# The last row of each partition of a final store, sent by nine small DMAs of 96 to 1 rows

## The chip, the cores and the metric

One core of a Trainium2 chip. The metric is device time in microseconds (us) of one execution, a median of several. All runs used here are fast, with a granted clock of 1.00. The experiments ran on two chips (6 and 11 in the record), each beside the kernel before on the same chip. A ratio is the mean time of one kernel's fast runs over that of the kernel before in the same rounds, so it is not quite the ratio of the medians quoted beside it.

## The reference

RMS normalisation with a gain and a ReLU, over 16,384 rows of 512 float32:

```python
def reference(x, gamma, eps):                       # x: 16 x 1024 x 512
    rms = np.sqrt(np.mean(x ** 2, axis=-1, keepdims=True) + eps)
    return np.maximum(x / rms * gamma, 0).astype(np.float32)
```

33.6 MB have to be read and 33.6 MB written, and little is computed on each element.

## The kernel before

The rows are cut into eight chunks of 4 MB. In a chunk each of 128 partitions (the rows of the memory on the chip) holds K = 16 neighbouring rows, so 32 KB lie together both in a partition and in the output. Six slots hold six chunks; the last two chunks reuse slots 0 and 1 after their stores have landed. SyncE issues every large load and store. ScalarE squares and sums, VectorE scales and clips in place. The parts that matter here:

```python
    K = 16
    nchunks = rows // K          # 8
    nslots = 6
    ov = out2.rearrange("(c p k) d -> c p k d", p=P, k=K)
    # ...
    def store(i):
        nc.sync.dma_start(out=ov[i], in_=slot_ap(i)).then_inc(sem_slot[i % nslots], 16)
    # ...
        for i in range(nchunks):
            nc.sync.wait_ge(done, per * (i + 1))
            store(i)
            # ... (load of the chunk that reuses a slot)
    # ... the end of the program: SyncE waits for every slot's last store
        nc.sync.reg_mov(landed, 64)
        for s in range(nchunks - nslots):
            nc.sync.wait_ge(sem_slot[s], landed)
```

A store here adds 16 to its semaphore (a counter on which an engine can wait): in the trace before, the last store shows 16 landings on it, the last at 159.88 us, 0.48 after the last of its packets had ended (159.40). I call the count that one DMA engine adds for one store an **increment**: in the records it is a packet of 4 bytes, 9 ns long, behind that engine's data.

## Time and profile before

| | before |
|---|---|
| device time, median of the first 3 runs | 162.86 us (162.81 to 163.07) |
| span of the profiled execution (its device time) | 160.9 us (162.69 us) |
| VectorE busy | 126.0 us |
| data moved, mean rate | 67.1 MB, 417 GB/s |
| last store issued / landed | 146.46 / 159.88 us |

The issue of the last store in the timeline (start, length, engine, line) took 0.33 us, where its data landed 13.4 us after its start:

```profile
146.46 0.33 SPq L87 DMA_DIRECT2D out_dram<-slots  x1
```

The DMA view of the stretch from 159.3 us to the end has one packet left, the increment of the engine that ends last:

```profile
DMA packets 1, 0.00 MB, mean 0 GB/s; under 512 B 1, under 2 KB 1, under 8 KB 1
```

"Under 512 B" counts increments here, since the data packets of this store have 32,768 bytes each. So the end is one engine's: its last data packet, its increment (over at 159.40 us), and then the 0.48 us until the increment lands. The prediction shows how the other fifteen lie before it.

### The profile page before, as it was taken

The page shows a single profiled execution, that of the slowest core. Times are in us where ns is not written, and L with a number is a line of the kernel's source. Part 1 is how long each engine was busy: PE and PEld are TensorE (multiplying, and loading weights), DVE is VectorE, ACT ScalarE, POOL GpSimd, SP SyncE. Part 2 cuts the span into 40 slices and gives each one's busy share as a digit, 9 for nine tenths or more (in the row PEclk, how much of TensorE's full clock was granted, in tenths as well). Part 3 has the DMA queues.
Part 4 walks back from the last instruction along what each step waited for, and adds up shares of the span by engine and source line. Part 5 has one row for each costly group of instructions (what it writes and reads, how often), then busy time and mean ns, then how long its engine had stood idle before and what let it go on. Part 6 is the DMA issues. An engine that isn't in the chain of part 4 may idle for free. (4 is left out here: it accounts for less than half of the span.)

```text
span 160.9 us, 1006 instructions
## 1 busy us (share of the span) xinstructions
DVE 126.0 (78%) x164; ACT 86.3 (54%) x273; POOL 0.2 (0%) x4
## 2 busy tenths in 40 slices
DVE  1103989898989899999999999999999999994000
ACT  3088929889988988988900198503994000000000
POOL 0000000000000000000000000000000000000000
DMA  5999999999999998999999999999999999999993
GB/s 155 434 432 415 521 391 391 513 399 391 489 424 391 481 432 367 415 391 489 424 391 489 424 391 448 464 391 440 456 407 432 456 415 424 464 415 424 464 407 138
DMA packets 2456, 67.12 MB, mean 417 GB/s; under 512 B 276, under 2 KB 276, under 8 KB 280
## 3 DMA queue, kind: packets, MB, share of 16 engines
q1 hardware_dynamic: 2448, 67.11, 97.6%
q10 hardware_dynamic: 8, 0.01, 0.0%
HBM read 33.56 MB, written 33.55 MB: 417 GB/s over the span
## 5 line engine op out<-in xcount | busy, mean ns | idle before, releaser
L124 ACT ACTIVATE junk<-slots 128x512 f32 x128 | 74.5, 582 | 30.6 <-ACTq L120 30.3
L148 DVE SCALAR_TENSOR_TENSOR slots<-slots,rstd,gamma_sb 128x512 f32 x128 | 86.2, 747 | 4.8 <-DVEq L145 4.8
L155 DVE TENSOR_SCALAR slots<-slots x16 | 36.7, 2294 | 2.4 <-DVEq L154 0.2
L124 ACT ACTIVATION_READ_ACCUMULATOR junk<-slots x128 | 23.9, 187 | 0.0
L142 DVE RECIPROCAL rstd<-rms x16 | 3.1, 196 | 6.3 <-DVEq L138 6.3
L131 ACT ACTIVATE rms<-ss,eps_sb x16 | 4.8, 301 | 3.0 <-ACTq L130 3.0
L135 DVE LOAD_MASK_SELECT gamma_sb<-gseed x1 | 0.0, 14 | 5.8 <-DMA gseed<-in_gamma_dram 5.8
L116 ACT ACT_TABLE_LOAD x1 | 1.3, 1283 | 2.8 <-issue 2.8
L109 DVE MEMSET gseed<- 128x512 f32 x1 | 0.5, 485 | 1.1 <-SPq L90 1.1
L135 DVE STREAM_SHUFFLE gamma_sb<-gseed 128x512 f32<-128x512 f32 x1 | 0.7, 715 | 0.0
L180 POOL MEMSET const-bfloat16-1.0<- 128x1 bf16 x1 | 0.1, 103 | 0.0
L180 POOL MEMSET const-uint8-127<- 128x1 uint8 x1 | 0.1, 102 | 0.0
L180 POOL MEMSET const-float32-0.0<- 128x1 f32 x1 | 0.1, 100 | 0.2 <-issue 0.2
L180 POOL MEMSET const-float32-1.0<- 128x1 f32 x1 | 0.1, 99 | 0.0
L110 DVE MEMSET eps_sb<- 128x1 f32 x1 | 0.1, 59 | 0.0
## 6 DMA issues: line engine op xcount, KB each, us to landing
out_dram<-slots SPq DMA_DIRECT2D x8, 4096.0 KB, 31.3
slots<-in_x_dram SPq DMA_DIRECT2D x7, 4096.0 KB, 30.3
slots<-in_x_dram SPq DMA_DIRECT2D x2, 2048.0 KB, 9.6
gseed<-in_gamma_dram ACTq DMA_DIRECT2D x1, 8.0 KB
```

Source lines behind the costliest of these rows:

```text
L109: nc.vector.memset(gseed, 0.0).then_inc(sem_z, 1)
L110: nc.vector.memset(eps_sb, eps).then_inc(sem_z, 1)
L116: nc.scalar.preload_act_table(ACTF.Sqrt)
L124: a = nc.scalar.activation(out=junk[:, j, :], in_=slots[:, bass.ds(base + j * d, d)], func=ACTF.Square, accum_out=ss[:, bass.ds(col + j, 1)])
L131: nc.scalar.activation(out=rms[:, bass.ds(col, G)], in_=ss[:, bass.ds(col, G)], func=ACTF.Sqrt, bias=eps_sb, scale=inv_d).then_inc(sq, 1)
L135: nc.vector.stream_shuffle(gamma_sb, gseed, [0] * 32)
L142: nc.vector.reciprocal(out=rstd[:, bass.ds(col, G)], in_=rms[:, bass.ds(col, G)]).then_inc(sv, 1)
L148: r = nc.vector.scalar_tensor_tensor(out=row, in0=row, scalar=rstd[:, bass.ds(col + j, 1)], in1=gamma_sb, op0=ALU.mult, op1=ALU.mult)
L155: nc.vector.tensor_scalar_max(out=blk, in0=blk, scalar1=0.0).then_inc(done, 1)
L180: nc = _bacc.Bacc("TRN2", target_bir_lowering=False, num_devices=1)
```

## The change

Its intent: some DMA engines end later than others, the last one at 159.40 us where the mean of the sixteen is 158.70. A transfer of a few rows can use a few engines only: in the trace before, gamma's load of four rows has four data packets and four increments. So one row of each partition is sent in small unequal stores, to give some engines more and others less. That all these stores take the same engines, in one order, each store as many as it has rows, was my assumption; the trace before does not show it. The engine numbers 0 to 15 (and "low", "high", "the fifth engine") in this document and in the recorded texts are places in that assumed order, the engine with most rows under the change first; no record carries a number.

```diff
+    parts = [(0, P, 0, K)]
+    cuts = [0, 96, 100, 107, 113, 118, 122, 125, 127, 128]
+    tail = [(0, P, 0, K - 1)] + [(a, b, K - 1, K) for a, b in zip(cuts[:-1], cuts[1:])]
+
     def store(i):
-        nc.sync.dma_start(out=ov[i], in_=slot_ap(i)).then_inc(sem_slot[i % nslots], 16)
+        for p0, p1, k0, k1 in (tail if i == nchunks - 1 else parts):
+            nc.sync.dma_start(out=ov[i][p0:p1, k0:k1, :],
+                              in_=slot_ap(i)[p0:p1, k0:k1, :]
+                              ).then_inc(sem_slot[i % nslots], 16)
 ...
-        nc.sync.reg_mov(landed, 64)
         for s in range(nchunks - nslots):
+            last = tail if s == nchunks - nslots - 1 else parts
+            nc.sync.reg_mov(landed, 48 + 16 * len(last))
             nc.sync.wait_ge(sem_slot[s], landed)
```

## The prediction

What neither a trace nor a run of this case showed is cut from the recorded text, and the cuts are marked. The sum came to 162.86 - 0.12 = 162.74 us. The rows for each engine (14, 13, 12, 11, 9, 8, 7, and nine times 6) are an estimate from the assumption above: the 96-row store gives six to each of sixteen engines, and the stores of 4, 7, 6, 5, 4, 3, 2 and 1 rows one more to each of that many. The -0.12 needs only the six rows, and that the slowest engine is one that gets no more than these.

> **What bounds the kernel now.** I read the page first, then the DMA queue's own waits, then narrow stretches at the end of the span. The page, its second, third and fourth part:
>
> ```profile
> span 160.9 us, 1006 instructions
> DVE 126.0 (78%) x164; ACT 86.3 (54%) x273; POOL 0.2 (0%) x4
> ...
> DMA  5999999999999998999999999999999999999993
> ...
> q1 hardware_dynamic: 2448, 67.11, 97.6%
> q10 hardware_dynamic: 8, 0.01, 0.0%
> HBM read 33.56 MB, written 33.55 MB: 417 GB/s over the span
> ## 4 chain that ended last, share of the span: by engine, by line
> DVE 1%; issue 0%
> ```
>
> The reader is to see that the DMA row is at 9 from the second slice to the last but one, that the transfers of one queue fill 97.6% of what sixteen engines have, and that no compute engine is above 78%. The chain of waits covers only 1% of the span: it stops at the last VectorE pass, because what ends after it is a transfer and not an instruction. The kernel is bound by moving 67.1 MB through sixteen DMA engines. The queue's own waits say how it ends:
>
> ```profile
> SPq L87 <- DVE slots L155: 105.2, 6, 26.5
> SPq L75 <- DMA out_dram<-slots: 33.0, 2, 24.2
> SPq L163 <- DMA out_dram<-slots: 12.4, 1, 12.4
> ```
>
> The columns are total us, times, longest. L163 is the wait for the slot of the last store, and it lasts 12.4 us. The timeline has the last store issued at 146.46 us; its landing is 13.4 us later by the page's list of issues, so at about 159.87, and the program closes about 1.0 us after. The last stretch by narrow windows (us from the span's start, length, busy of DVE, ACT, POOL, clock, DMA share, GB/s; a transfer packet counts where it starts):
>
> ```profile
> 157.00:157.70 0.70, 0.00 (x0) 0.00 (x0) 0.00 (x0) 1.00 1.41 609
> 157.70:157.90 0.20, 0.00 (x0) 0.00 (x0) 0.00 (x0) 1.00 0.76 328
> 157.90:158.10 0.20, 0.00 (x0) 0.00 (x0) 0.00 (x0) 1.00 0.00 0
> 158.10:158.30 0.20, 0.00 (x0) 0.00 (x0) 0.00 (x0) 1.00 0.38 164
> ```
>
> 609 GB/s for 0.70 us is 426 KB, so 13 packets of 32,768 bytes; the next window has two and the one from 158.10 has one. These are the sixteen last packets, one for each engine. Thirteen engines start theirs within 0.7 us, two are late, one is later still. That last one decides the end. The packet records, followed from one packet to the next (each begins 4 ns before its predecessor ends, so sixteen chains can be drawn through the run, with some ambiguity), put the sixteen ends at 158.37 to 158.83, then 159.01, 159.03 and 159.40. Their mean is 158.70. So **perfect levelling of the load is worth at most 159.40 - 158.70 = 0.70 us, 0.4% of 162.86.** The three last chains also began last (2.59, 2.94 and 2.94 us, most others 1.96 to 2.24): the lag of the start is carried to the end, since the engines never run dry in between.
>
> [...] gamma's load of four rows shows 8 packets on q10, four of 2,048 bytes and four of the semaphore, and five updates of its semaphore. The records don't number the engines, so no view shows that they are the lowest four. [...] Before, an increment of 4 bytes takes 9 ns and the next packet starts 4 to 6 ns after it started, so it doesn't hold up the engine here; it lands some 0.33 us after its packet on most engines, 0.48 us on the slowest. [...]
>
> **The change part by part.** The 4 MB store of 128 pieces of 32 KB, eight for each engine, becomes one of 128 pieces of 30,720 bytes and nine that carry row 15 of each partition in pieces of 2,048 bytes.
>
> *Issue.* Nine more issues. Seven loads were issued in 3.60 us at the start, 0.51 us each, so ten stores take about 5 us and are out by 151.6. Previous stores keep the engines on until about 148.7, and the new main part alone lasts 8 x 1.13 = 9.1 us after that, to about 157.8. The small ones are queued some 6 us before an engine reaches them: hidden.
>
> *Who carries what.* 96 rows give six to each of sixteen engines. [...] So the engines hold 14, 13, 12, 11, 9, 8, 7 rows, and nine of them 6, in place of 8 everywhere (sum 128). [...]
>
> *Cost of a row.* A packet of 32,768 bytes takes 1,213 ns in the records and one of 16,384 takes 611: 36.7 ns for 1,000 bytes and about 9 ns fixed, of which 4 overlap. A row inside a large packet is 75 ns. Gamma's packets of 2,048 bytes took 84 ns, 80 with the overlap. So each small row costs 5 ns more than inside a large one, and each further increment 5 ns.
>
> *An engine with six rows*: two rows less, -150 ns; six small pieces, +30; one more increment, +5: **-0.12 us**. *Engine 0*: +6 x 75 = 450, 14 x 5 = 70, nine increments 45: +0.57. Engine 1 +0.48, engine 2 +0.39, engine 3 +0.31, engine 4 +0.14, engine 5 +0.05, engine 6 -0.04.
>
> *The end.* The four chains that carried gamma ended at 158.51, 158.62, 158.66 and 158.74. If they are engines 0 to 3, the worst pairing gives 158.74 + 0.57 = 159.31. The slowest chain, if it is one of engines 7 to 15, ends at 159.40 - 0.12 = 159.28, and lands later after its last packet (0.48 against 0.33 us). So it stays last, and the end moves from 159.87 to about 159.75. The waits after it cost nothing: they are on the same landing, with one more register move. Sum: 162.86 - 0.12 = 162.74.
>
> **Rivals.** *The slowest engine is a low one.* Against: the three late chains have no gamma packet, so none of them is among the four that carried it. For: engine 4 could be one; then +0.14, 163.0.
>
> *The increments stall an engine.* Engine 0 gets ten in a row, nine of them a row or so apart, where before at least eight packets lay between. If each waits out the 0.33 us of the landing before the next row may go, engine 0 loses about 9 x 0.33 = 3 us less the 0.1 us by which it leads: up to 165.5, still under 2%. Against: after an increment today the next packet begins without a gap. But the case of many close ones is not in the trace, so I leave it some weight.
>
> *Small pieces to HBM are slow.* If a 2 KB write took twice its 84 ns, engines 7 to 15 would lose 0.5 us and gain 0.15, engine 0 would lose over 1 us: about 163.2 to 163.7. Gamma's 84 ns speak against it, though that was a read.
>
> *All hidden.* The lag of an engine comes from the start and varies from run to run; the three times before differ by 0.26 us, twice the gain. Then the median shows nothing.
>
> **Range and chances.** The gain is bounded by 0.70 us on paper and 0.12 by the working; the losses that I can name reach 0.3 to 3 us with small weight. I take 162.75 us, 162.5 to 163.2: below by the noise, above by part of the second and third rival. Over 2% faster would need 3.3 us, over four times what levelling can give: 0.01. Slower by 3.3 us needs the stall at full size and something else: 0.02.
>
> **What would show it.** Right: the waits of L163's kind end about 0.1 us earlier; one more q1 packet row of about 128 small packets, near 84 ns each; the last chains still the late starters; the increments without gaps. The ten issues end before 152 us. Wrong: a chain with many small packets that ends last and has gaps after its increments (the stall); small packets of 150 ns or more (slow writes); the issues still running when the main part is through (then the sequencer would set the end); a late starter with more than six small packets (the low-engine rival).

## The result, and the profile after

163.34 us (162.97 to 163.47, 6 runs) against 162.91 us (162.75 to 163.23, 6 runs): ratio 1.0023, 95% interval 1.0009 to 1.0037. A loss of some 0.4 us, within 2%, where a gain of 0.12 us was worked out. The page after, the lines that answer to those of before:

```profile
span 161.6 us, 1015 instructions
DVE 126.0 (78%) x164; ACT 86.3 (53%) x273; POOL 0.2 (0%) x4
...
DMA  5999999999999999999999999999999999999991
...
q1 hardware_dynamic: 2624, 67.11, 97.2%
...
HBM read 33.56 MB, written 33.55 MB: 415 GB/s over the span
```

Compute is the same to the tenth of a microsecond, the bytes are the same, the engines are as full. What differs is the end. The queue's own waits and the timeline of its issues, after:

```profile
SPq L205 <- DMA out_dram<-slots: 4.2, 1, 4.2
```

```profile
146.42 9.09 SPq L95 DMA_DIRECT2D out_dram<-slots  x10
```

The wait at the end shrank from 12.4 to 4.2 us, which is no gain: SyncE now spends 9.09 us on ten issues, 0.91 each, where I had estimated 0.51, and so begins to wait later. The issues are through at 155.51 us. The wait is still for a DMA, so the sequencer doesn't set the end. The DMA view from 159.3 us on, after:

```profile
DMA packets 9, 0.01 MB, mean 6 GB/s; under 512 B 4, under 2 KB 4, under 8 KB 9
```

Nine packets in place of one: five rows of 2 KB and four increments. By the packet records all nine belong to one chain (a chain is one engine's packets, each linked to the one that starts as it ends); the next chain ended at 159.20 us. This chain's whole share is readable because it is alone at the end: six small rows from the 96-row store, then three rows each with an increment of its own. **Nine small rows** is what the fifth engine (engine 4 of 0 to 15) holds in the prediction's list of rows, and no other does; the chain itself shows one row more than the eight of before. Its packets end at 159.77 us, 0.38 later than the last chain before.

The list rests on my assumption, and this trace agrees with it as far as it goes. There are 48 increments more than before (324 packets under 512 B against 276), the sum 16 + 4 + 7 + 6 + 5 + 4 + 3 + 2 + 1. If its packet records are linked so that every chain has six small rows and an increment first, with steps within 1 ns of the usual ones, the 32 rows of the eight smallest stores lie on seven or eight of the sixteen chains; the list's own counts are one such linking among others. Which engines these are, no record says.

The landings say the rest. The trace's records of the last store's semaphore give the arrival of each increment; for this chain (us):

```
increment packet ends    159.52   159.60   159.69   159.77    0.086 apart
increment lands          160.02   160.20   160.39   160.57    0.186 apart
delay                      0.50     0.60     0.70     0.80
```

(The pairing is by order; packets and landings of a semaphore carry no engine number.) Before, the same delay of the last increment was 0.48 us. So the span grew by 0.38 us of packets and 0.32 us of landing, together 0.70. This single pair flatters the kernel before, whose profiled run was below its median; the medians differ by 0.43 us.

The same records hold a second late series. Landings at 159.72, 159.90, 160.08 and 160.25 us lie 0.175 to 0.177 apart; by this spacing they too are one engine's, though all chains but the slowest had ended their packets by 159.20. So a faster engine with many close increments would by itself have ended the program at 160.25, 0.37 later than the 159.88 of before.

### The profile page after: what moved, and what is told of

It reads as the page before. It is cut to its first block, busy times and chain, and to the rows that moved or that the text cites. A ratio compares the mean times of both kernels' runs of the same rounds, so it can differ in the third digit from the quotient of the medians.

```text
span 161.6 us, 1015 instructions
## 1 busy us (share of the span) xinstructions
DVE 126.0 (78%) x164; ACT 86.3 (53%) x273; POOL 0.2 (0%) x4
```

## The experiments

**Theory A**: the engine that ends last is one that the change loads more, so its extra bytes and pieces cost time. **Theory B**: A, and besides, closely spaced increments of one engine land only every 0.19 us or so, and the last one lands late. **Theory C**: it is noise of a start that varies. Theory D came up later. All runs compare with the kernel before on the same chip; for the four runs of the second session (low4, low4prev, even8x4, low4x2prev) nine of its ten times are those of the first, eight minutes earlier.

| run | what the last store's (or, "store but one", the seventh's) end looks like | median us | before | ratio (95% interval) |
|---|---|---|---|---|
| again | the change | 163.19 | 162.73 | 1.0030 (1.0017 to 1.0044) |
| one128 | row 15 in one store | 162.68 | 162.73 | 0.9999 (0.9985 to 1.0012) |
| even8 | row 15 in eight stores of 16 rows | 163.70 | 162.73 | 1.0059 (1.0045 to 1.0073) |
| prev | the change's pieces, store but one | 162.91 | 162.73 | 1.0011 (0.9997 to 1.0025) |
| low4 | 96 rows, then eight times 4 | 163.33 | 162.73 | 1.0041 (1.0027 to 1.0055) |
| low4prev | the same, store but one | 162.70 | 162.73 | 1.0008 (0.9989 to 1.0028) |
| even8x4 | as even8, four rows each | 163.95 | 162.73 | 1.0075 (1.0061 to 1.0089) |
| low4x2prev | two rows: 112, then four times 4; store but one | 162.81 | 162.73 | 1.0005 (0.9991 to 1.0018) |
| even8s | as even8, every eighth partition | 163.69 | 162.83 | 1.0053 (1.0040 to 1.0067) |
| even8x4s | as even8x4, every eighth partition | 162.86 | 162.83 | 1.0004 (0.9990 to 1.0018) |
| bytes65 | row 15 in stores of 65 and 63 rows | 163.20 | 162.83 | 1.0023 (1.0010 to 1.0037) |
| rows4 | rows 12 to 15, one store each | 162.83 | 162.83 | 0.9998 (0.9985 to 1.0012) |

All were correct.

### The change once more

No edit.

> The change itself once more, with an interval. Theory A (bytes and pieces: the engine that ends last is one of those that the change loads more, it carries nine small rows in place of eight): +0.14 us over the kernel before. Theory B (A, and each small piece with an increment of its own is slow to land, some 0.19 us apart on the slowest engine where its packets are 0.086 apart, so four such pieces add some 0.3 us more after the last packet): +0.45 us. Theory C (the first result was noise of a start that varies): within 0.1 us. The slowest chain again has nine small rows and ends last under A and B.

+0.46 us between the medians. C falls: the loss repeats in another session and its interval excludes zero. The slowest chain again holds nine small rows, and its last two increments land 0.180 and 0.186 us after the ones before them. This and all pairings below go by order and spacing.

### Small rows by themselves

```diff
-    cuts = [0, 96, 100, 107, 113, 118, 122, 125, 127, 128]
+    cuts = [0, 128]
```

> Row 15 of the last store goes by a single store of 128 rows: eight small rows on each engine, no engine loaded more, one further increment. A: eight rows at 5 ns more and one increment, +0.05 us. B: the same +0.05, and the last increment lands up to 0.1 us later at most. C: 0. If small rows to HBM were slow by themselves, +0.3 us or more.

No difference (-0.05 us by medians, interval about -0.24 to +0.20). All 128 small packets took 84 ns. So 2 KB pieces to HBM took no longer than gamma's reads of 2 KB (84 ns), and the prediction's third rival is gone. The slowest chain's last increment landed 0.47 us after its packet: one increment behind eight small rows landed as fast here as the one behind large packets before (0.48).

### Increments by themselves

```diff
-    cuts = [0, 96, 100, 107, 113, 118, 122, 125, 127, 128]
+    cuts = list(range(0, 129, 16))
```

(written out as [0, 16, ..., 128])

> Row 15 goes by eight stores of 16 rows, one row on each engine from each: the load is as even as before, but every engine has eight single rows each with its increment. A: eight rows at 5 ns and eight increments at 5 ns, +0.08 us. B: eight increments landing 0.1 us later each than the packets pass, +0.7 to 0.9 us, the last landings 0.19 us apart. C: within 0.1.

+0.97 us, with the load as even as before. A falls as the whole story, B's number is met and slightly passed. Narrow windows of this run, in the columns of the prediction's last fence:

```profile
159.00:159.70 0.70, 0.00 (x0) 0.00 (x0) 0.00 (x0) 1.00 0.25 85
159.70:161.00 1.30, 0.00 (x0) 0.00 (x0) 0.00 (x0) 1.00 0.00 0
```

From 159.70 no packet starts any more; the last one of all ends at 159.60. Yet the semaphore's last increments arrive at 160.56, 160.75 and 160.93 us, the last two 0.186 and 0.187 after the one before. That is 1.34 us from the last packet to the last landing. **The engines' packet rows look done, and the program is not**: what it waits for is not in the busy time of any engine.

### The change's pieces one store earlier

```diff
-        for p0, p1, k0, k1 in (tail if i == nchunks - 1 else parts):
+        for p0, p1, k0, k1 in (tail if i == 6 else parts):
...
-            last = tail if s == nchunks - nslots - 1 else parts
+            last = tail if s == 0 else parts
```

> The same ten pieces, but of the last store but one, so that the engines still have the whole last store behind them and no small increment lands last. A: +0.14 us, since the nine rows and the increments still hold up the slowest engine. B: also about +0.14 us; the 0.3 us of late landing are gone, so it is some 0.3 us faster than the change. C: 0, like the change.

+0.18 us by medians, between -0.05 and +0.41 by the interval: it holds the 0.14 of the prediction's first rival, and zero too. The slowest chain again has nine small rows, here in the store but one, and the DMA view from 159.3 us on is as before the change:

```profile
DMA packets 1, 0.00 MB, mean 0 GB/s; under 512 B 1, under 2 KB 1, under 8 KB 1
```

The semaphore of this store reached its count at 150.81 us in the trace, its last two gaps being 0.193 us, against about 150.2 to 150.4 in the runs where this store was whole. So the late landing is there too, and it costs nothing, because the whole last store runs behind it. Compared with the change itself in the same rounds, 163.19 - 162.91 = 0.28 us are saved, with no overlap between the two sets of five times: the landing part.

### Fewer rows on the slow engine, more on four others

```diff
-    cuts = [0, 96, 100, 107, 113, 118, 122, 125, 127, 128]
+    cuts = [0, 96, 100, 104, 108, 112, 116, 120, 124, 128]
```

> Row 15 of the last store goes by one store of 96 rows and eight of four: [...] A (bytes alone): the slowest chain ends 0.12 us earlier, -0.1 us. B: the slowest chain ends 0.12 us earlier, but the four low engines, with six rows more and eight single rows with an increment each, pass their last packets at about 159.3 us and land the last of them some 0.33 + 8 x 0.1 us later, at about 160.4: +0.5 us, set by the low engines.

Four rows go over four engines in gamma's load (four data packets, four increments); that all eight stores of four take the same four was assumed. By that estimate these four, the low ones, hold 6 + 8 = 14 small rows and all others 6.

+0.60 us. The slow chain (six small rows, one small increment) now ends its packets at 159.35; another chain ends at 159.46. The last landing is at 160.56, with 0.18 to the one before. If the slow chain's single small increment took the usual 0.48, it landed near 159.83 (an estimate), long before. So by all signs other engines set the end, those with the single rows: the landing rhythm is not a fault of the slow engine. It is 0.17 to 0.18 us on these engines as well.

The same in the store but one (edits of the last two together):

> The same pieces of the last store but one. A and B alike: no small increment lands last, the slowest chain has two rows less, -0.1 us; were the low four engines to become the last ones, 0. If increments held up an engine's packets and not only their landing, +0.3 us or more.

162.70 against 162.73 us. Five of six runs lie at 162.49 to 162.77 and one at 163.55, so neither the gain of 0.1 us nor its absence is shown. That increments hold up the packets by 0.3 us is not seen in these five; the interval, which the sixth widens, runs from about -0.18 to +0.46 and doesn't exclude it.

A candidate for a gain, with pieces twice as large and half as many:

```diff
-    tail = [(0, P, 0, K - 1)] + [(a, b, K - 1, K) for a, b in zip(cuts[:-1], cuts[1:])]
+    tail = [(0, P, 0, K - 2), (0, 112, K - 2, K)] + [(a, a + 4, K - 2, K) for a in range(112, P, 4)]
```

(and the two edits that move it to the store but one)

> The best candidate: the store but one sends rows 14 and 15 by one store of 112 partitions and four of four partitions with 4 KB each. [...] A and B: slowest chain -0.13 us, time -0.1 us against the kernel before; a lag of other engines may leave it at 0.

The -0.13 us is an estimate from the same assumption: shared over sixteen engines, 112 pieces of two rows are seven each, so 14 rows in place of 16, and the four small stores give four of the engines eight rows more.

162.81 us: no gain is seen (interval about -0.15 to +0.29). I found no version that clearly beats the kernel before.

### Larger pieces between increments

```diff
-    tail = [(0, P, 0, K - 1)] + [(a, b, K - 1, K) for a, b in zip(cuts[:-1], cuts[1:])]
+    tail = [(0, P, 0, K - 4)] + [(a, a + 16, K - 4, K) for a in range(0, P, 16)]
```

> Eight stores of 16 rows for the last piece as in the even one, but each carries four rows (8 KB) of a partition, so an engine's packets take 0.305 us from one increment to the next, more than the 0.186 us in which increments land. B: the landings keep up, +0.05 to +0.1 us. If each increment cost 0.1 us whatever its piece: +0.9 us again, as with one row. If the number of stores or their issue were the cost: +0.9 us too.

+1.22 us: a miss for B, as it stood, and by its number this run seems to say that the count of increments is all. The packets say otherwise. Of 128 packets of 8 KB, 41 took over 320 ns, up to 1,191, with a mean of 409 where 309 is the usual. The windows show a dent:

```profile
155.00:156.00 1.00, 0.00 (x0) 0.00 (x0) 0.00 (x0) 1.00 0.92 393
156.00:157.00 1.00, 0.00 (x0) 0.00 (x0) 0.00 (x0) 1.00 1.25 336
157.00:158.00 1.00, 0.00 (x0) 0.00 (x0) 0.00 (x0) 1.00 0.75 254
158.00:159.00 1.00, 0.00 (x0) 0.00 (x0) 0.00 (x0) 1.00 0.88 287
```

From 156 to 157 us the busy share is high and the rate low: the packets there are long, not missing. Eight stores of 16 neighbouring partitions went over sixteen engines each in the run with single rows (even8: 128 increments more than before, 404 packets under 512 B against 276), so it may be that sixteen engines read neighbours at the same time here. That these get in each other's way is **theory D**, a possible cause that B's arithmetic had left out. Two runs test whether the choice of partitions matters, each with every eighth partition in place of 16 neighbours:

```diff
+    tail = [(slice(0, P), 0, K - 1)] + [(slice(a, P, 8), K - 1, K) for a in range(8)]   # even8s
+    tail = [(slice(0, P), 0, K - 4)] + [(slice(a, P, 8), K - 4, K) for a in range(8)]   # even8x4s
```

> As the even one (eight stores of 16 rows, one row for each engine from each), but each store takes every eighth partition in place of 16 neighbours. Theory B (increments land 0.186 us apart on an engine, whatever rows they follow): +0.9 us as with the neighbours. Theory D (16 neighbouring partitions, read by sixteen engines at once, get into each other's way): much less than +0.9, about +0.1 us.

+0.86 us by medians: with single rows the choice of partitions hardly matters (+0.86 against +0.97), so D doesn't explain the loss there, while B's number fits.

> As the even one with four rows each, but every eighth partition. There 42 of 128 packets of 8 KB took up to 1.19 us in place of 0.309. D: those packets become even and short, and +0.1 us stays (pieces of 0.315 us between increments). B says nothing on the packets; its part is the increments, which keep up: +0.1 us if the packets are short. If many increments alone cost the time, +0.9 us or more again.

+0.03 us. Same number of stores, same number of increments, same bytes per piece as in the run that lost 1.22 us; only the partitions differ, and with them the places in HBM (the chip's main memory), which lie 256 KB apart within a store in place of 32. So the choice of partitions is shown to matter here; whether the reading side is at fault, as D says, or the writing side, no run separates. The issues are no rival: they ended at 157.94 us here, later than the 156.99 of the run that lost.

Its windows:

```profile
155.00:156.00 1.00, 0.00 (x0) 0.00 (x0) 0.00 (x0) 1.00 0.88 377
156.00:157.00 1.00, 0.00 (x0) 0.00 (x0) 0.00 (x0) 1.00 1.09 410
157.00:158.00 1.00, 0.00 (x0) 0.00 (x0) 0.00 (x0) 1.00 0.94 328
158.00:159.00 1.00, 0.00 (x0) 0.00 (x0) 0.00 (x0) 1.00 0.73 279
```

The rate stays higher from 156 to 158 us. The mean packet took 345 ns; 31 of 128 were still over 320, so the cure is not complete. The last increment landed 0.48 us after its packet, as before the change: with at least 0.31 us between increments, they keep up. Eight further increments on every engine cost nothing that can be seen here (interval about -0.16 to +0.29), where a piece takes longer than the 0.19 us of a landing.

### Bytes by themselves

```diff
-    cuts = [0, 96, 100, 107, 113, 118, 122, 125, 127, 128]
+    cuts = [0, 65, 128]
```

> Row 15 of the last store by two stores, of 65 and 63 rows. [...] A: if the slowest chain is the fifth engine it now has twelve small rows, four more than before: 4 x 75 + 12 x 5 + 10 = +0.37 us, and no late landing to speak of (+0.1 at most). [...]

That the fifth engine would hold twelve small rows was assumed from a way in which 65 and 63 rows would be shared among the engines. The run shows it in part only.

+0.37 us, the expected number. From 159.3 us to the end the DMA view has

```profile
DMA packets 7, 0.01 MB, mean 7 GB/s; under 512 B 1, under 2 KB 1, under 8 KB 7
```

six rows and one increment, 80 ns from row to row, alone on one chain, and the increment lands 0.46 us after its packet, on time. Six rows without an increment between them belong to one store. Spread evenly over sixteen engines, 63 or 65 rows would give an engine four or five at most, so at least one of the two stores was not spread evenly, and the slowest chain got more than an even share of it. The loss agrees: +0.37 us. How many engines each store used, that the slow chain held twelve rows, and that its engine is the one with nine rows under the change (on another chip), is not shown.

### Increments with eight rows between them

```diff
-    tail = [(0, P, 0, K - 1)] + [(a, b, K - 1, K) for a, b in zip(cuts[:-1], cuts[1:])]
+    tail = [(0, P, 0, K - 4)] + [(0, P, k, k + 1) for k in range(K - 4, K)]
```

> The last four rows of the last store by four stores of one row of all 128 partitions: even load, eight small rows (0.64 us) between increments, 32 small rows on each engine. A and B: 32 rows at 5 ns less the eight pieces' own, four increments: +0.16 us, landings keep up. If an increment cost 0.1 us whatever lies between: +0.55 us.

0.00 us between the medians (interval about -0.24 to +0.20, which holds the expected +0.16). Four more increments with 0.64 us between them (an estimate: eight rows, 80 ns from one to the next) cost nothing that can be seen; the +0.55 expected if each cost 0.1 us lies outside.

## Why the prediction was wrong

*The bound* was right: DMA fills the span, compute doesn't matter (126.0 us of VectorE in both traces), and the end is one engine's, though the landing of its increment and not its last packet. The limit of 0.4% on what levelling could give was not put to the test, since no run gained; "within 2%" was right.

*Issue*: hidden, as said, though each issue took 0.91 us where 0.51 was estimated, and they ended at 155.51 where "before 152 us" was to be seen. The margin to the first small packet (157.68 us) was 2.2 us in place of about 6.

*Who carries what*, which rested on an assumption, agrees with the counts of the trace after (48 increments more, nine rows on the slow chain), and *the cost of a row* was right. Small packets took 84 ns, followed by the next after 80; a load taken as twelve rows, by assumption, cost +0.37 us as computed (interval +0.16 to +0.60). One sum slipped: by the same terms engine 6 comes to -75 + 35 + 10 = -30 ns, so -0.03 and not -0.04, which changes nothing.

**The step that failed is the end**: "The slowest chain, if it is one of engines 7 to 15, ends at 159.40 - 0.12 = 159.28 ... So it stays last". The slowest chain is, by its nine rows, one that the change loads more, the fifth engine's by the list. The trace before gave no engine numbers; gamma's load ruled out only the four engines that carried it, and I gave the fifth as a rival at +0.14 us and took the other case for the sum. That term is -0.12 in the working, and in its place the runs show a load: +0.18 with the landings hidden (the pieces moved one store earlier; the interval just reaches zero) and +0.37 with the load taken as twelve rows.

**A second term was missing from the sum**: the landing of the increments. The rival "the increments stall an engine" was half right. The packets aren't stalled: increments and rows follow each other without a gap (in the slow chain after, each row starts 6 ns after the increment before it). But the landings come 0.17 to 0.19 us apart on one engine while packets come 0.086 apart, so on the slow chain the fourth of four close increments lands 0.80 us after its packet, not 0.48. That is the other 0.3 us; moving the pieces ahead of other work took away 0.28. This term alone would have broken the step: engine 0 was to end at 159.31 at worst and land about 0.33 later, but the second late series landed at 160.25, after the 159.75 forecast for the slowest, whichever engine that was. I weighed the two rivals as alternatives, each with a number of its own (163.0; up to 165.5), when both came true at once: 0.14 + 0.3 = 0.44, and 0.43 was measured, 0.46 the second time.

Also doubtful, and not shown by the traces, is "the lag of the start is carried to the end". In the repeated run of the change, some 70 packets of the slow chain, as I linked it, were longer than the usual for their size, in the next chains 12 to 15. That speaks for time lost throughout the run; but chains can't be followed through the whole trace without ambiguity, so why this engine is late stays open. Open too is why landings keep 0.18 us: the runs show the rhythm, that with single rows it doesn't depend on the choice of partitions, and that it is hidden behind larger pieces or other work, not what makes it.

## What to carry to other kernels

Before shifting load between DMA engines, find out which one is late by a load that only some of them can carry, and read its count of packets at the end of the trace. At the very end of a program, count the semaphore increments that each engine has to land close together: here, increments 0.086 us apart on an engine made the last landing later (0.80 us after its packet, not 0.48), while increments 0.31 us or more apart (+0.03 and 0.00 us), or the same small pieces ahead of another large transfer (+0.18, with zero in its interval), cost little or nothing. Where the change lies between the two was not measured. And a limit computed first (here 0.70 us for perfect levelling) tells whether the work is worth it.
